# Every third weight remainder of a decoder layer computed on GpSimd instead of VectorE

## The chip, the cores and the metric

The kernel runs on one core of a Trainium2 chip. The metric is the device time of one execution in microseconds (us); less is better. The engines are named as the profile names them: PE (TensorE, matmuls), PEld (its weight loads), DVE (VectorE), ACT (ScalarE), POOL (GpSimd) and SP (SyncE, which issues DMAs here).

## What is computed

One decoder layer on 512 tokens with 2048 channels, all in float32:

```python
xn = rms_norm(x, norm1_g);  proj = xn @ w_in + b_in
mixed = concatenate([conv_group(...), swa_group(...)])     # convolution branch, sliding-window attention
x = x + mixed @ w_out
x = x + peer(rms_norm(x, norm2_g), ...)

def peer(xn, ...):     # 8 heads pick 16 of 16384 one-neuron experts each, for every token
    experts, gates = top-16 of the product keys
    h = einsum("cd,chkd->chk", xc, peer_u[experts])
    a = gelu(h) * gates
    return einsum("chk,chkd->cd", a, peer_v[experts])
```

The expert layer (`peer`) takes most of the time.

## The kernel before, in words

**Two ways through the expert layer.** For 352 of the tokens the kernel computes all 16384 experts densely: a sweep multiplies the activations with `peer_u`, the result is multiplied by gates that are zero for the experts not chosen, and a fold multiplies that with `peer_v` and adds into `acc`. For the other 160 tokens it fetches the chosen expert rows with indirect DMAs that GpSimd issues (`gather`, 320 of them, 1 MB each), and DVE works each fetched row off with one long instruction over 128x2048 elements: L842 for `peer_u`, L859 for `peer_v`. The gathers have three buffers in turn (`grow` twice, and `yrow` or `xrow`), so that gather n may start only when the DVE step of gather n-3 has ended. `step` spreads the gathers over the dense tiles, by number and not by time.

**Weight units.** All dense weights come in 628 units of 128x1024 float32 (512 KB), in a fixed order (`specs`). For each unit `stream` has SP load it (`w_raw`, two buffers; an own queue), ACT round it to the matmul's float32r (`w_hi`, three buffers), and DVE subtract that from the original (`w_lo`, three buffers). So a unit's `w_raw` buffer is free for the unit after next when its `w_lo` is done, and its `w_hi` buffer when PE has used it. PE multiplies each unit with 24 matmuls in the order high weight by high activation, high weight by low activation, low weight by high activation; it needs `w_hi` at the unit's first matmul and `w_lo` at the third. `unit` asks for one unit ahead, and the two instructions of the split stand under a raised priority (400) of the tile scheduler, which sets the order of all instructions on each engine from a simulated timeline.

**Stages of the dense part.** Sweeps 0 to 8 (units 116 to 259) store their results in DRAM. For groups 9 to 15 a sweep of 16 units is followed at once by its fold of 16 units (`fold_group`); the first of these folded groups begins at unit 260. Behind group 15 the stored groups 0 to 8 are folded, 16 units each: `prepare` loads the stored results (`Hb`) and gates (`Gb`), and queues their gating (`gated`, L965, and the split of the gated values at L171 and L172) into the fold of the group before. After each pair of output blocks DVE adds two PSUM banks into `acc` (L989).

Of the kernel before, what the change touches and what calls it, by code (L numbers as in the profile page):

```python
# [9 lines left out]
FT = mybir.dt.float32  # L10
# [4 lines left out]
OP = mybir.AluOpType  # L15
# [11 lines left out]
AHEAD = 9  # L27
START = 10
END = 250.0
PUMP = 5.4  # L30
CONV_K = 31
HD, NQ = 64, 16
NK, PH, TOPK = 128, 8, 16
# [2 lines left out]
C_N1, C_N2, C_CB, C_LG, C_LB, C_BA, C_BG, C_CW = 0, 16, 32, 40, 48, 56, 64, 72  # L36
N_PAR = C_CW + 8 * CONV_K
R_B, R_SK, R_QG, R_KG = 0, 1280, 1296, 1360
# [21 lines left out]
def hymba_layer(ctx: ExitStack, tc: tile.TileContext, xT, pos, par, row, wi, wo, wq, sk, ut, un, vt, vn,  # L60
                out_t, out_r, dbg=None):
    nc = tc.nc
# [18 lines left out]
    def later(cost, fn, *a, low=False):  # L81
        queues[low].append((cost, fn, a))
# [11 lines left out]
    def drain(low=True):  # L94
        for q in queues[:1 + low]:
            while q:
                _, fn, a = q.popleft()
                fn(*a)
# [26 lines left out]
    def stream(upto):  # L125
        while nxt[0] < min(upto, len(specs)):
            i = nxt[0]
            nxt[0] += 1
            raw = raws[-1][0].tile([128, 1024], FT, name="w_raw", bufs=raws[-1][1])
            with tc.high_priority(offset=400 if i >= 4 else 0):  # L130
                nc.sync.dma_start(raw, specs[i])
            hi = ring.tile([128, 1024], FR, name="w_hi", bufs=3)
            lo = ring.tile([128, 1024], FR, name="w_lo", bufs=3)
            with tc.high_priority(offset=400):
                nc.scalar.activation(hi, raw, AF.Copy)  # L135
                nc.vector.tensor_tensor(lo, raw, hi.bitcast(FT), op=OP.subtract)  # L136
            units[i] = (hi, lo)

    def unit(ahead=1):
        i = nxt[1]  # L140
        nxt[1] += 1
        stream(i + 1 + ahead)
        return units.pop(i)
# [19 lines left out]
    def par_col(base, c):  # L163
        return P[:, base + c:base + c + 1]
# [72 lines left out]
    for c in range(KC):  # L237
        if c % 4 == 0:
            stream(c // 4 + 1)
        xr = px.tile([128, T], FT, name="xr", bufs=4)  # L240
        nc.sync.dma_start(xr, xT[c])
        nc.scalar.activation(xh[:, c], xr, AF.Copy, scale=par_col(C_N1, c))
        nc.vector.scalar_tensor_tensor(xl[:, c], xr, par_col(C_N1, c), xh[:, c].bitcast(FT), op0=OP.mult,
                                       op1=OP.subtract)
        if c == 0:
            nc.scalar.activation(ssq, xr, AF.Square)
        else:
            sq = px.tile([128, T], FT, name="sq", bufs=2)
            nc.scalar.activation(sq, xr, AF.Square)
            nc.vector.tensor_tensor(ssq, ssq, sq, op=OP.add)  # L250
# [30 lines left out]
    def conv_chunk(c, h):  # L281
        first = [True]

        def tap(k):
            w = par_col(C_CW, c * CONV_K + k)
            if k == 0:
                nc.vector.tensor_scalar(mix_c[:, c], h[:, :T], w, par_col(C_CB, c), op0=OP.mult, op1=OP.add)
            else:
                nc.vector.scalar_tensor_tensor(mix_c[:, c], h[:, k:k + T], w, mix_c[:, c], op0=OP.mult, op1=OP.add)  # L289
        for k in range(CONV_K):  # L290
            later(0.66, tap, k, low=True)
# [192 lines left out]
    def glu_group(g):  # L484
# [15 lines left out]
        nc.scalar.activation(tg, tg, AF.Sigmoid, bias=par_col(C_BG, g))  # L500
        h = pa_.tile([128, CONV_K - 1 + T], FT, name="h", bufs=2)
        nc.gpsimd.memset(h[:, :CONV_K - 1], 0.0)
        nc.vector.scalar_tensor_tensor(h[:, CONV_K - 1:], ta, par_col(C_BA, g), tg, op0=OP.add, op1=OP.mult)
        conv_chunk(g, h)
# [279 lines left out]
    for h in range(PH):  # L784
# [6 lines left out]
        for u in range(4):  # L791
            hi, lo = unit()
# [123 lines left out]
    def step(first, us):  # L916
        tick[0] += 1
        if tick[0] > START:
            gather_until(int((tick[0] - START) * STEPS / (END - START)) + 1, first)
        pump(us)  # L920
# [18 lines left out]
    for e in range(8 * AHEAD):  # L939
# [3 lines left out]
        if e % 4 == 3:  # L943
            nc.scalar.dma_start(H[e // 4], gl)
        step(first, PUMP)
    drain()
# [149 lines left out]
```

## Time and profile before

| what | value |
|---|---|
| median of three runs | 2863.24 us (2862.2 to 2864.12) |
| the profiled execution | 2863.08 us, of which the span from first to last instruction is 2861.3 us |
| PE busy | 2811.3 us, 98% |
| DVE busy | 2368.2 us, 83% |
| POOL busy | 471.7 us, 16% |
| largest group on DVE | `w_lo`, 628 instructions, 772.1 us |

The span is the profile's own clock; the 1.8 us between it and the execution's time lie around the program. A matmul's rows overlap (each lasts some 0.32 us, and the next starts 0.16 us after it), so a busy PE is read here from its gaps: an idle time of PE or PEld with the name of what ended it.

### The profile page before, as it was taken

To read this page: it belongs to the slowest core of one execution; us is meant where nothing else is said; L and a number is where in the kernel's file an instruction comes from. 1 tells how busy PE (TensorE), PEld (TensorE's weight loads), DVE (VectorE), ACT (ScalarE), POOL (GpSimd) and SP (SyncE) were. 2 spreads that over 40 slices of the span, in tenths; PEclk is the share of its full clock that TensorE was granted. 3 is DMA by queue.
4 is the path that set the end of the run, shared out by engine and by line. 5 is a ranking of instruction groups with operands and counts; after the bars stand their busy time and mean duration, and the time that the engine had idled before them with its cause. 6 is when DMAs were issued, how large, how long until landed. Compare 5 with 4: busy or idle time off the path is not lost. (4 is left out here: it accounts for less than half of the span.)

```text
span 2861.3 us, 43542 instructions
## 1 busy us (share of the span) xinstructions
PE 2811.3 (98%) x16995; PEld 2688.8 (94%) x16995; DVE 2368.2 (83%) x3586; ACT 1214.2 (42%) x1879; POOL 471.7 (16%) x337
## 2 busy tenths in 40 slices
PE   8999999999999999999999999999999999999999
PEld 8998877788899999999999999999999999999999
DVE  7888996569999887777787878878888899997984
ACT  5666434343343787666332333333333333333332
POOL 0000000000002222212212222222222223222320
PEclk9999999999999999999999999999999999999999
DMA  5222332523249999899998989898898999998994
GB/s 174 75 67 74 115 100 85 170 93 136 89 157 345 325 325 339 311 341 339 349 351 321 343 313 359 335 336 336 326 344 323 372 361 350 354 366 329 358 347 147
DMA packets 204207, 764.00 MB, mean 267 GB/s; under 512 B 18593, under 2 KB 70945, under 8 KB 160417
## 3 DMA queue, kind: packets, MB, share of 16 engines
q1 hardware_dynamic: 103584, 378.66, 36.7%
q0 software_dynamic: 46080, 335.56, 31.0%
q10 hardware_dynamic: 54336, 47.00, 5.0%
q8 instruction: 133, 2.18, 0.3%
q14 instruction: 74, 0.60, 0.1%
HBM read 716.42 MB, written 44.70 MB: 266 GB/s over the span
## 5 line engine op out<-in xcount | busy, mean ns | idle before, releaser
L135 ACT ACTIVATE w_hi<-w_raw 128x1024 fp32r<-128x1024 f32 x628 | 666.0, 1061 | 1277.7 <-PE mm L981 536.1
L136 DVE TENSOR_TENSOR w_lo<-w_raw,w_hi 128x1024 fp32r<-128x1024 f32 x628 | 772.1, 1233 | 276.6 <-ACT w_hi L135 275.4
L932 PE MATMUL mm<-nl,w_hi 128*128 128x352 f32 x2048 | 668.2, 326 | 0.0
L930 PE MATMUL mm<-nh,w_hi 128*128 128x352 f32 x2048 | 664.9, 325 | 1.0 <-ACT w_hi L135 1.0
L979 PE MATMUL mm<-ah,w_hi 128*128 128x352 f32 x2048 | 658.4, 323 | 7.4 <-DVE acc L989 7.4
L933 PE MATMUL mm<-nh,w_lo 128*128 128x352 f32 x2048 | 664.0, 325 | 0.0
L981 PE MATMUL mm<-al,w_hi 128*128 128x352 f32 x2048 | 660.3, 323 | 0.0
L982 PE MATMUL mm<-ah,w_lo 128*128 128x352 f32 x2048 | 645.0, 323 | 12.7 <-DVE w_lo L136 12.5
L982 PEld LDWEIGHTS mm<-ah,w_lo 128*128 128x128 f32 x2048 | 380.9, 188 | 18.0 <-DVE w_lo L136 17.9
L979 PEld LDWEIGHTS mm<-ah,w_hi 128*128 128x128 f32 x2048 | 384.0, 188 | 9.2 <-DVE acc L989 7.6
L930 PEld LDWEIGHTS mm<-nh,w_hi 128*128 128x128 f32 x2048 | 385.3, 188 | 1.5 <-ACT w_hi L135 1.3
L933 PEld LDWEIGHTS mm<-nh,w_lo 128*128 128x128 f32 x2048 | 385.4, 188 | 0.1
L932 PEld LDWEIGHTS mm<-nl,w_hi 128*128 128x128 f32 x2048 | 384.8, 188 | 0.1
L981 PEld LDWEIGHTS mm<-al,w_hi 128*128 128x128 f32 x2048 | 384.8, 188 | 0.0
L826 POOL DMA_INDIRECT grow<-un,idx x86 | 121.3, 1411 | 898.9 <-DVE grow L842 591.3
L859 DVE SCALAR_TENSOR_TENSOR yrow<-grow,h,yrow 128x2048 f32<-128x2048 f32 x107 | 251.4, 2349 | 1.5 <-DMA grow<-vn,idxb 1.4
L842 DVE SCALAR_TENSOR_TENSOR grow<-grow,xrow 128x2048 f32<-128x2048 f32 x107 | 244.6, 2286 | 0.8 <-DMA grow<-un,idxb 0.8
L989 DVE TENSOR_TENSOR acc<-acc,mm 128x352 f32<-128x352 f32 x240 | 118.8, 521 | 87.4 <-PE mm L982 87.3
L826 POOL DMA_INDIRECT grow<-vn,idx x85 | 125.4, 1475 | 391.5 <-DVE yrow L859 381.6
L289 DVE SCALAR_TENSOR_TENSOR mix_c<-h,par,mix_c 128x512 f32<-128x512 f32 x240 | 173.8, 750 | 1.6
L859 DVE SCALAR_TENSOR_TENSOR yrow<-xrow,h,yrow 128x2048 f32<-128x2048 f32 x53 | 124.6, 2351 | 0.0
L842 DVE SCALAR_TENSOR_TENSOR yrow<-yrow,xrow 128x2048 f32<-128x2048 f32 x53 | 121.2, 2286 | 2.9 <-DMA xrow<-XB 2.9
(274 smaller groups left out, 3979.3 us busy)
## 6 DMA issues: line engine op xcount, KB each, us to landing
w_raw<-ut SPq DMA_DIRECT2D x256, 512.0 KB
w_raw<-vt SPq DMA_DIRECT2D x256, 512.0 KB
w_raw<-wi SPq DMA_DIRECT2D x52, 512.0 KB
G<-gt ACTq DMA_DIRECT2D x22, 1024.0 KB
Gb<-G SPq DMA_DIRECT2D x16, 1408.0 KB
w_raw<-wo SPq DMA_DIRECT2D x32, 512.0 KB
w_raw<-wq SPq DMA_DIRECT2D x32, 512.0 KB
H<-gl ACTq DMA_DIRECT2D x18, 704.0 KB
```

The costliest lines, as they stand in the source:

```text
L135: nc.scalar.activation(hi, raw, AF.Copy)
L136: nc.vector.tensor_tensor(lo, raw, hi.bitcast(FT), op=OP.subtract)
L289: nc.vector.scalar_tensor_tensor(mix_c[:, c], h[:, k:k + T], w, mix_c[:, c], op0=OP.mult, op1=OP.add)
L826: i = nc.gpsimd.indirect_dma_start(out=g, out_offset=None, in_=src, in_offset=bass.IndirectOffsetOnAxis(ap=at, axis=0))
L842: nc.vector.scalar_tensor_tensor(g, g, 1.0, rows["x"], op0=OP.mult, op1=OP.mult, accum_out=h3[:, k:k + 1])
L859: nc.vector.scalar_tensor_tensor(y, g, h3[:, k:k + 1], y, op0=OP.mult, op1=OP.add)
L930: m = nc.tensor.matmul(bank, hi[:, s], nh[:, k, :TD], start=k == 0, stop=False)
L932: nc.tensor.matmul(bank, hi[:, s], nl[:, k, :TD], start=False, stop=False)
L933: nc.tensor.matmul(bank, lo[:, s], nh[:, k, :TD], start=False, stop=k == KC - 1)
L979: m = nc.tensor.matmul(banks[j], hi[:, ws], ah[:, ee], start=ee == 0, stop=False)
L981: nc.tensor.matmul(banks[j], hi[:, ws], al[:, ee], start=False, stop=False)
L982: nc.tensor.matmul(banks[j], lo[:, ws], ah[:, ee], start=False, stop=ee == 7)
```

## The change

From unit 260 on, the subtraction that makes `w_lo` is issued to GpSimd instead of DVE for every unit whose number divides by three: units 261, 264, ..., 627, which are 123 of the 368 left. Inputs, output and buffers stay the same. The constant is the number of units ahead of the first folded group (116 units of projections, then 16 for each of 9 sweeps).

```diff
+POOL_LO = 116 + 16 * AHEAD
@@ stream
             with tc.high_priority(offset=400):
                 nc.scalar.activation(hi, raw, AF.Copy)
-                nc.vector.tensor_tensor(lo, raw, hi.bitcast(FT), op=OP.subtract)
+                eng = nc.gpsimd if i >= POOL_LO and i % 3 == 0 else nc.vector
+                eng.tensor_tensor(lo, raw, hi.bitcast(FT), op=OP.subtract)
```

Lines behind the first edit move by one, behind the second by two: L826 of before is L828 of the changed kernel, L859 is L861, L965 is L967, L989 is L991.

On POOL, in the folds of the stored groups (units 534 to 546), only gathers stand in a row before; the number behind a name is that of the buffer's use.

```order
L826 DMA xrow_23355<-vn,idx_5227 128x2048
L826 DMA grow_23425<-vn,idx_5227 128x2048
L826 DMA grow_23428<-vn,idx_5227 128x2048
L826 DMA xrow_23498<-vn,idx_5227 128x2048
L826 DMA grow_23568<-vn,idx_5227 128x2048
```

In the changed kernel the same stretch of POOL reads:

```order
L138 TENSOR_TENSOR w_lo_23253<-w_raw_23250,w_hi_23252 128x1024
L828 DMA xrow_23355<-vn,idx_5227 128x2048
L828 DMA grow_23425<-vn,idx_5227 128x2048
L138 TENSOR_TENSOR w_lo_23366<-w_raw_23363,w_hi_23365 128x1024
L828 DMA grow_23428<-vn,idx_5227 128x2048
L828 DMA xrow_23498<-vn,idx_5227 128x2048
L138 TENSOR_TENSOR w_lo_23469<-w_raw_23466,w_hi_23468 128x1024
L828 DMA grow_23568<-vn,idx_5227 128x2048
```

Between two moved subtractions stand about two gathers, and POOL takes all of them in order.

On DVE the scheduler has also put the remaining instructions into another order. Around unit 538 (`w_lo_23396`) in a fold of a stored group, before:

```order
L136 TENSOR_TENSOR w_lo_23366<-w_raw_23363,w_hi_23365 128x1024
L965 TENSOR_TENSOR Hb_23788<-Hb_23788,Gb_23784 128x352 x4
L989 TENSOR_TENSOR acc_13638<-acc_13638,mm_23291 128x352
L989 TENSOR_TENSOR acc_13638<-acc_13638,mm_23292 128x352
L859 SCALAR_TENSOR_TENSOR yrow_17709<-xrow_23355,h3_7322,yrow_17709 128x2048
L965 TENSOR_TENSOR Hb_23790<-Hb_23790,Gb_23784 128x352 x4
L136 TENSOR_TENSOR w_lo_23396<-w_raw_23393,w_hi_23395 128x1024
```

and in the changed kernel, DVE at the same place:

```order
L991 TENSOR_TENSOR acc_13638<-acc_13638,mm_23291 128x352
L991 TENSOR_TENSOR acc_13638<-acc_13638,mm_23292 128x352
L861 SCALAR_TENSOR_TENSOR yrow_17709<-xrow_23355,h3_7322,yrow_17709 128x2048
L138 TENSOR_TENSOR w_lo_23396<-w_raw_23393,w_hi_23395 128x1024
L967 TENSOR_TENSOR Hb_23788<-Hb_23788,Gb_23784 128x352 x4
L967 TENSOR_TENSOR Hb_23790<-Hb_23790,Gb_23784 128x352 x4
```

The subtraction of unit 537 has left DVE, and that of unit 538 now stands ahead of the eight gating instructions.

Where the folds of the stored groups begin (units 474 to 476), DVE before:

```order
L136 TENSOR_TENSOR w_lo_21094<-w_raw_21091,w_hi_21093 128x1024
L172 TENSOR_TENSOR al_20908<-Hb_20909,ah_20907 128x352
L859 SCALAR_TENSOR_TENSOR yrow_17709<-grow_21050,h3_7322,yrow_17709 128x2048
L172 TENSOR_TENSOR al_20908<-Hb_20909,ah_20907 128x352
L172 TENSOR_TENSOR al_20908<-Hb_20911,ah_20907 128x352 x4
L989 TENSOR_TENSOR acc_13638<-acc_13638,mm_21059 128x352
L136 TENSOR_TENSOR w_lo_21134<-w_raw_21131,w_hi_21133 128x1024
L989 TENSOR_TENSOR acc_13638<-acc_13638,mm_21060 128x352
L859 SCALAR_TENSOR_TENSOR yrow_17709<-xrow_21053,h3_7322,yrow_17709 128x2048
L136 TENSOR_TENSOR w_lo_21164<-w_raw_21161,w_hi_21163 128x1024
```

and in the changed kernel:

```order
L861 SCALAR_TENSOR_TENSOR yrow_17709<-grow_21050,h3_7322,yrow_17709 128x2048
L174 TENSOR_TENSOR al_20908<-Hb_20909,ah_20907 128x352
L174 TENSOR_TENSOR al_20908<-Hb_20911,ah_20907 128x352 x4
L991 TENSOR_TENSOR acc_13638<-acc_13638,mm_21059 128x352
L861 SCALAR_TENSOR_TENSOR yrow_17709<-xrow_21053,h3_7322,yrow_17709 128x2048
L138 TENSOR_TENSOR w_lo_21134<-w_raw_21131,w_hi_21133 128x1024
L991 TENSOR_TENSOR acc_13638<-acc_13638,mm_21060 128x352
L138 TENSOR_TENSOR w_lo_21164<-w_raw_21161,w_hi_21163 128x1024
```

Unit 474's subtraction (`w_lo_21094`) is gone from DVE, and unit 475's (`w_lo_21134`) now stands behind one more of the long gather steps.

## Rows read from the trace of the kernel before

**Rows 1.** The page's first part: busy us, share of span and instructions by engine.

```profile
PE 2811.3 (98%) x16995; PEld 2688.8 (94%) x16995; DVE 2368.2 (83%) x3586; ACT 1214.2 (42%) x1879; POOL 471.7 (16%) x337
```

**Rows 2.** Busy time in five stretches: length, PE, PEld, DVE, ACT, POOL, clock, DMA.

```profile
1400.00:2240.00 840.00, 833.84 (x5206) 832.39 (x5205) 674.43 (x671) 280.36 (x344) 182.29 (x143) 1.00 0.90 338
1800.00:1900.00 100.00, 100.00 (x627) 100.00 (x627) 81.15 (x84) 33.62 (x42) 21.58 (x17) 1.00 0.90 340
2240.00:2275.00 35.00, 31.65 (x191) 30.25 (x191) 35.00 (x40) 9.38 (x10) 11.91 (x6) 1.00 0.95 370
2275.00:2700.00 425.00, 414.34 (x2560) 410.15 (x2559) 377.88 (x396) 133.68 (x163) 125.23 (x71) 1.00 0.92 354
2700.00:2861.00 161.00, 156.76 (x963) 154.50 (x961) 115.29 (x109) 45.28 (x50) 26.16 (x19) 1.00 0.71 261
```

**Rows 3.** Waits from 1400 to 2240 us: us in total, times, longest.

```profile
PEld mm L979 <- DVE acc L989: 7.6, 5, 2.0
```

**Rows 4.** Waits from 2240 to 2275 us.

```profile
PEld mm L982 <- DVE w_lo L136: 3.2, 4, 1.7
PEld mm L979 <- ACT w_hi L135: 1.5, 1, 1.5
```

**Rows 5.** Waits from 2275 to 2700 us.

```profile
DVE acc L989 <- PE mm L982: 39.0, 22, 6.7
PEld mm L982 <- DVE w_lo L136: 14.7, 14, 1.6
DVE w_lo L136 <- ACT w_hi L135: 6.6, 9, 2.2
DVE yrow L859 <- DMA grow<-vn,idxb: 1.4, 2, 1.2
```

**Rows 6.** Groups on DVE, 2240 to 2861 us: busy, mean ns, idle before.

```profile
L136 DVE TENSOR_TENSOR w_lo<-w_raw,w_hi 128x1024 fp32r<-128x1024 f32 x154 | 186.3, 1224 | 26.6 <-ACT w_hi L135 26.5
L859 DVE SCALAR_TENSOR_TENSOR yrow<-grow,h,yrow 128x2048 f32<-128x2048 f32 x65 | 152.8, 2351 | 1.5 <-DMA grow<-vn,idxb 1.4
L989 DVE TENSOR_TENSOR acc<-acc,mm 128x352 f32<-128x352 f32 x157 | 78.1, 522 | 57.6 <-PE mm L982 57.6
L859 DVE SCALAR_TENSOR_TENSOR yrow<-xrow,h,yrow 128x2048 f32<-128x2048 f32 x32 | 75.3, 2353 | 0.0
L172 DVE TENSOR_TENSOR al<-Hb,ah 128x352 fp32r<-128x352 f32 x71 | 32.3, 522 | 0.0
L965 DVE TENSOR_TENSOR Hb<-Hb,Gb 128x352 f32<-128x352 f32 x64 | 29.5, 529 | 0.0
```

**Rows 7.** Timeline about 1797 us: start, length, instruction, [idle before, releaser].

```profile
1796.48 1.23 DVE L136 TENSOR_TENSOR w_lo<-w_raw,w_hi 128x1024 fp32r<-128x1024 f32 x1 [0.40 <-ACT w_hi L135]
...
1803.18 0.19 PEld L933 LDWEIGHTS mm<-nh,w_lo 128*128 128x128 f32 x1
```

**Rows 8.** Timeline about 2497 us, a late unit.

```profile
2496.79 1.83 DVE L965 TENSOR_TENSOR Hb<-Hb,Gb 128x352 f32<-128x352 f32 x4
...
2499.81 0.30 PEld L982 LDWEIGHTS mm<-ah,w_lo 128*128 128x128 f32 x2 [0.66 <-DVE w_lo L136]
```

**Rows 9.** Groups on POOL, the whole span: two MEMSET sizes.

```profile
L855 POOL MEMSET yrow<- 128x2048 f32 x1 | 1.8, 1812 | 10.9 <-DMA out_r<-yrow 10.9
L348 POOL MEMSET vh<- 128x1024 f32 x1 | 1.0, 954 | 40.0 <-PE rowstat L262 40.0
```

**Rows 10.** Timeline about 2315 us, POOL and DVE.

```profile
2314.47 2.35 DVE L859 SCALAR_TENSOR_TENSOR yrow<-xrow,h,yrow 128x2048 f32<-128x2048 f32 x1
2314.71 2.93 POOL L826 DMA_INDIRECT grow<-vn,idx  x1 [4.45 <-DVE yrow L859]
```

**Rows 11.** Timeline about 2434 us, POOL and the DVE instruction behind.

```profile
2433.84 0.94 POOL L826 DMA_INDIRECT grow<-vn,idx  x1 [3.71 <-DVE yrow L859]
2435.84 0.52 DVE L989 TENSOR_TENSOR acc<-acc,mm 128x352 f32<-128x352 f32 x1 [2.27 <-PE mm L982]
```

**Rows 12.** Waits of SP's queue, 2240 to 2861 us.

```profile
SPq L131 <- DVE w_lo L136: 432.6, 150, 8.7
```

## The prediction

> **What bounds the kernel now.** I read the page's first part, then the stretches, then who waited for whom in each, and only then single places. PE is busy for 2811.3 of 2861.3 us [rows 1]. The stretch from 1800 to 1900 us shows what a PE without gaps looks like: 627 matmuls in 100.00 us [rows 2], 0.16 us each, so a unit of 24 takes 3.83 us and three units take 11.5 us. Nothing done on another engine makes that faster; the change can only take away gaps of PE, or add some. The reader should see how few there are behind 1400 us, where the moved units begin: 7.6 us for `acc` [rows 3], 3.2 and 1.5 us from 2240 to 2275 us [rows 4], 14.7 us in 14 waits from 2275 to 2700 us [rows 5]. From 2700 us on DVE makes PE wait no more; its last gaps belong to the program's end. The waits that carry the name of `w_lo` sum up to 17.9 us in 18 waits, 0.6% of the time. That is about the ceiling of a gain.
>
> They all lie in the folds of the stored groups. In the folded groups ahead, `w_lo` is ready long before its use: at 1797 us it starts right when ACT's `w_hi` ends, is done at 1797.71, and PE first loads it at 1803.18 [rows 7], 5.5 us later. From 2240 to 2275 us DVE is busy for all of 35.00 us, from 2275 to 2700 us for 377.88 of 425 us, 89% [rows 2]. Its queue is in order, and a `w_lo` that stands behind gating or a gather step there comes late: at 2497 us four gating instructions, 1.83 us, run right ahead of unit 538's `w_lo`, and PE waits 0.66 us [rows 8].
>
> **What the change removes.** DVE loses one `w_lo` of 1224 ns [rows 6] in three units: 123 of them, 37 in the 425 us (425 / 11.5). With nothing added, DVE's 377.88 us there would be 333.
>
> **What it adds on GpSimd.** The trace has no GpSimd instruction with two inputs. The nearest rows are the two MEMSETs, 954 ns for 1024 elements in a partition and 1812 ns for 2048 [rows 9]: 858 ns for each 1024 elements that go one way, and 96 ns around. Two inputs read one after the other give 96 + 2 x 858 = 1.8 us, two inputs and the output one after the other 2.7 us. I take 2.2 us, between the ends, since no row tells which is nearer. The Trainium skill has a figure, in "GPSIMD Engine Reference", section 3.1: 4497 ns for an addition over 2048 elements, from which half, 2.25 us, is an estimate; by it the sum would not change.
>
> POOL works 125.23 of the 425 us now [rows 2], so 37 x 2.2 = 81 us more fit. What counts is its order: a moved subtraction stands behind a gather that may wait for a DVE step, and gathers stand behind a subtraction that waits for `w_hi`. Reading each moved unit against the trace of before (the later of `w_hi`'s end and the end of the gather ahead of it, plus 2.2 us) leaves at most units some 4 us before PE needs them; for about five of the 49 or so units from 2240 to 2800 us it leaves nothing or up to a microsecond. I take +1 us for those. Gathers move back by up to 2.2 us or what the subtraction waits; DVE waited only 1.4 us for gathered data in the late stretch [rows 5], so their cover is thin but there, and I take nothing for them. SP's next load waits for `w_lo` as well, 150 times [rows 12]; at 1797 us a GpSimd subtraction would end 1 us after DVE's. That load is for the unit after next, which PE reaches two units or 7.7 us later, so nothing is taken for it either.
>
> **What it costs DVE.** Does a GpSimd instruction that reads two tensors hold DVE up? The trace shows the other direction. A gather issue takes 0.94 us when DVE is idle [rows 11] and 2.93 us when it starts 0.24 us into a long gather step; that step ends at 2316.82, and the issue ends 0.82 us after that [rows 10]. So a GpSimd instruction is held while a DVE instruction with two SBUF inputs runs. How a long reading instruction of GpSimd holds DVE is not shown; the ends are nothing, and its whole length. I take the whole length, for the share of time in which DVE has such an instruction: all groups of [rows 6] but `acc` (whose second input is in PSUM), 186.3 + 152.8 + 75.3 + 32.3 + 29.5 = 476 of 621 us, 77%. Then one moved subtraction costs DVE 0.77 x 2.2 = 1.7 us and saves 1.22: +0.5 us net, with ends of -1.2 and +1.5 (2.7 without any cover). Times 37 that is +18 us: DVE at 396 of 425 us, 93%.
>
> The Trainium skill speaks against the change here: "SBUF — State Buffer", the practical consequences in its table of ports, says that a DVE instruction with two SBUF inputs and a GpSimd instruction that reads SBUF exclude each other, and that whichever comes second is blocked until the first has ended. The trace agrees in the one direction that it shows, 2.93 against 0.94 us. By the rule the sum is the one below; without it, it is the first rival's.
>
> **What the new order does.** DVE's order in the late stretch changes by more than the missing instructions. Adding up the DVE work ahead of each remaining `w_lo` in both orders, with the durations of [rows 6], the eleven late units from 2275 to 2700 us that stay on DVE fare so: ten stand earlier by 0.9 to 5.7 us, mostly by one gather step (2.35 us) or a little more, one stands where it stood. The place at unit 538 is of this kind: the eight gating instructions now come behind its `w_lo`. The other three late units go to GpSimd. Against that, a half to one net microsecond of blocking in a run of DVE between two idle times (31 idle times in 425 us, one in 13.7 us, so about one GpSimd instruction in each run) rarely eats 2.35 us. So of the 14.7 us I count 14 as gone.
>
> Three other units (491, 550, 554) stand later by 2.3 to 6.6 us and had slack of 2.3 to 5.5 us: +2 us. Units nearly late before get the 0.5 us on top: +1 us. In the opening part, 2240 to 2275 us, DVE has no idle time, and units 475 and 479 each get one gather step of 2.35 us more ahead of them, while two or three blocked subtractions cost 0.5 us net each. PE waits once for both (the second delay falls into the first): +3 us, on top of the 3.2 that stay.
>
> The waits of 7.6 us for `acc` [rows 3] come from loads of the residual; they stay.
>
> **Sum.** -14 (late units from 2275 to 2700 us) + 3 (opening part) + 2 (units put later) + 1 (nearly late) + 1 (GpSimd's own) = -7 us. The profiled execution took 2863.08 us, 0.16 us under the median, so the forecast is 2856 us.
>
> **Rivals.** *No blocking.* If DVE runs on beside GpSimd, every moved subtraction is a gain of 1.2 us for DVE: the opening part costs +1 instead of +3, the nearly late units nothing and the units put later +1: -14 + 1 + 1 + 1 = -11 us, and with half of the 3.2 us of [rows 4] gone as well, about -13: 2850 us. For it speaks that the rows show only GpSimd waiting; against it that the held issue shows a shared resource.
>
> *The relief is eaten.* The net +0.5 us falls on units that have no slack, mostly in long runs of DVE without idle time, where four GpSimd instructions add 2 us: half of the 14 us stays, and the sum is 0: 2863 us, within 6 us either way. For it speaks that DVE stays at 93%.
>
> *DVE becomes the bound from 2275 to 2700 us* (the slower side). DVE has 47 us to spare there, 1.27 us for each of the 37 subtractions. If one costs more than that net, that is over 2.5 us of blocked DVE each, as with a GpSimd instruction of 2.7 us or more and no cover, DVE needs all of the 425 us, and the idle times in which it waits for PE (39.0 us [rows 5]) can't all be filled. With 2.7 us, full blocking adds 1.5 x 37 = 55 us, 8 more than are free; if a quarter of the 47 us can't be filled, PE waits 20 us instead of 14.7, and with the opening part's +5 and late GpSimd units the time is about 2875 us; a GpSimd instruction of 3 us would give near 2890. For it speaks that GpSimd's duration is unmeasured; against it that the early idle time and the new order give some back.
>
> *The change doesn't do what it says*: the built program has 123 subtractions on POOL, so this is out.
>
> **Chances.** Forecast (3 to 11 us faster) 0.32; no blocking 0.18; relief eaten 0.27; DVE as the bound 0.23. 0.2% is 5.7 us, about what a measurement of this kernel can tell from no change. Of the forecast's 0.32 some 0.28 lie beyond that on the fast side and 0.04 within; relief eaten lies within but for 0.03 on the slow side; no blocking is fast, 0.18. So faster 0.46, within 0.28, slower 0.26. The range reaches from the no-blocking case with something to spare to the point where DVE is just the bound: 2846 to 2877 us. The forecast's own range is 2852 to 2860 us.
>
> **What would show it.** POOL should have 123 subtractions of about 2.2 us, and some longer by what a DVE instruction ahead of them still had to run. DVE's long gather steps or `w_lo` should at times last up to 2.2 us more, or start late behind nothing; if all keep 2.35 and 1.22 us, there is no blocking. The waits of PE for `w_lo` from 2275 to 2700 us should fall from 14.7 to some 4 us, and those in the opening part rise from 3.2 to about 6. I am wrong if waits for GpSimd's `w_lo` show in the folded groups ahead of 2240 us, where 5.5 us should cover everything, if DVE waits for gathers by more than 10 us, or if DVE's idle time from 2275 to 2700 us is used up.

## The result, and the profile after

The changed kernel takes 2898.97 us (median of four executions, 2892.07 to 2902.36) beside 2862.72 us of the kernel before on the same chip: a ratio of 1.0126, with an interval of 1.0111 to 1.014. It is 36 us slower. The forecast was 2856 us, faster, with a range up to 2877 us; both its sign and its range were wrong. The profiled execution took 2897.86 us, its span is 2896.0 us, 34.7 us over the span of before.

The first part of the page, busy us by engine, answers to [rows 1]:

```profile
PE 2828.0 (98%) x16995; PEld 2705.3 (93%) x16995; DVE 2383.0 (82%) x3463; ACT 1210.5 (42%) x1879; POOL 863.7 (30%) x460
```

DVE issues 123 instructions fewer and is busy for 15 us *more*. PE is busy for 17 us more at the same 16995 matmuls. Neither can come from the work itself, which is the same.

Where the time goes is seen best over the same work, since a kernel that has fallen behind does other work in the same microseconds. The matmuls of the stretches of [rows 2] (1400 to 2240 us, 2240 to 2275, 2275 to 2700, and from there on) are found again by counting matmuls from the start. In the changed kernel they take these stretches (columns as there):

```profile
1402.30:2242.90 840.60, 835.25 (x5206) 833.93 (x5205) 669.32 (x591) 274.40 (x335) 429.52 (x214) 1.00 0.89 337
2242.90:2291.80 48.90, 36.34 (x191) 35.21 (x190) 44.56 (x46) 13.37 (x18) 18.86 (x11) 0.86 0.83 316
2291.80:2732.90 441.10, 420.36 (x2561) 417.24 (x2560) 391.19 (x358) 133.68 (x163) 219.79 (x105) 0.98 0.90 336
2732.90:2896.00 163.10, 157.47 (x962) 154.33 (x960) 112.03 (x97) 44.87 (x50) 70.20 (x32) 1.00 0.71 257
```

The folded groups take 0.6 us more than before, the opening part 48.9 instead of 35 us, the late stretch 441 instead of 425, the end 163 instead of 161. Some 2 us of the 34.7 lie ahead of 1402 us, where GpSimd has not begun its first subtraction (1407.0 us).

The waits of PE's weight loads in the opening part and in the late stretch (columns as in [rows 3]: us in total, times, longest):

```profile
PEld mm L984 <- DVE w_lo L138: 8.8, 3, 5.5
PEld mm L981 <- ACT ah L173: 4.9, 1, 4.9
...
PEld mm L984 <- DVE w_lo L138: 20.8, 8, 4.8
PEld mm L984 <- POOL w_lo L138: 3.1, 3, 1.4
```

Against [rows 4] (4.7 us) the opening part now has 13.7 us, and the late stretch 23.9 us against the 14.7 of [rows 5]. The shape changed too: fourteen waits of at most 1.6 us became eight for DVE's `w_lo`, the longest 4.8 us, and three for GpSimd's. The end has 1.8 us for `w_lo`, where before it made PE wait for nothing. The folded groups have 6.7 us against 7.6 [rows 3], none of it for `w_lo`. All in all the waits for operands behind 1400 us rose from 27.0 to 46.2 us, by 19.2 us.

That leaves 15 of the 34.7 us. The stretches of time (columns as in [rows 2]) around seven of the longer waits show the larger part of them:

```profile
1537.40:1540.80 3.40, 3.38 (x11) 3.38 (x12) 2.62 (x3) 0.00 (x0) 0.00 (x0) 0.50 1.04 422
2247.40:2254.20 6.80, 5.86 (x20) 5.88 (x21) 6.80 (x12) 2.79 (x4) 1.73 (x1) 0.50 0.79 285
2278.10:2284.90 6.80, 5.32 (x18) 5.32 (x19) 4.82 (x4) 0.00 (x0) 3.77 (x2) 0.50 0.97 378
2332.70:2339.50 6.80, 5.72 (x19) 5.72 (x20) 4.75 (x4) 0.00 (x0) 2.70 (x2) 0.50 0.84 316
2397.50:2400.90 3.40, 3.03 (x10) 3.04 (x11) 3.40 (x5) 0.00 (x0) 0.00 (x0) 0.51 0.99 347
2476.10:2479.50 3.40, 3.40 (x13) 3.40 (x13) 2.73 (x2) 0.00 (x0) 1.53 (x1) 0.51 0.98 377
2595.50:2598.90 3.40, 2.79 (x9) 2.80 (x10) 3.40 (x3) 0.00 (x0) 0.00 (x0) 0.50 0.99 400
```

In these seven stretches, 34.0 us together, TensorE was granted half its clock (0.50: 1.2 instead of 2.4 GHz). Each begins during or right behind a wait of PE of 2.3 to 5.5 us. At half the clock the matmuls follow each other every 0.29 us instead of 0.16. The seven stretches hold 100 of them: 100 x 0.13 = 13 us. The kernel before has no such stretch behind 1400 us; its longest wait there is 2.0 us [rows 3], and its granted clock reads 1.00 in every stretch of [rows 2].

So the 34.7 us are 19.2 of waits, 13 of matmuls at half the clock, and 2.5 that I don't assign, nearly all of it the 2 us ahead of the first moved unit.

**What makes `w_lo` late.** The added group on POOL and the groups on DVE behind 1400 us (busy us, mean ns of one, idle before):

```profile
L138 POOL TENSOR_TENSOR w_lo<-w_raw,w_hi 128x1024 fp32r<-128x1024 f32 x123 | 365.4, 2971 | 385.4 <-ACT w_hi L136 384.7
```

```profile
L138 DVE TENSOR_TENSOR w_lo<-w_raw,w_hi 128x1024 fp32r<-128x1024 f32 x244 | 327.4, 1349 | 90.5 <-ACT w_hi L136 81.9 <-issue 8.5
L861 DVE SCALAR_TENSOR_TENSOR yrow<-grow,h,yrow 128x2048 f32<-128x2048 f32 x107 | 285.2, 2666 | 9.1 <-DMA grow<-vn,idx 7.2 <-DMA yrow<-YB 1.0 <-DMA grow<-vn,idxb 0.7
L861 DVE SCALAR_TENSOR_TENSOR yrow<-xrow,h,yrow 128x2048 f32<-128x2048 f32 x53 | 139.2, 2627 | 1.9 <-DMA xrow<-vn,idx 1.6
L991 DVE TENSOR_TENSOR acc<-acc,mm 128x352 f32<-128x352 f32 x232 | 113.2, 515 | 88.6 <-PE mm L984 88.3
L967 DVE TENSOR_TENSOR hv<-hv,Gb 128x352 f32<-128x352 f32 x56 | 60.1, 1075 | 7.8 <-ACT hv L936 7.7
L174 DVE TENSOR_TENSOR al<-hv,ah 128x352 fp32r<-128x352 f32 x56 | 44.0, 787 | 19.8 <-ACT ah L173 19.8
L967 DVE TENSOR_TENSOR Hb<-Hb,Gb 128x352 f32<-128x352 f32 x72 | 42.3, 649 | 7.6 <-DMA Gb<-G 7.6
```

Against [rows 6], `w_lo` went from 1224 to 1349 ns, the gather steps from some 2350 to 2666 and 2627, `Hb` from 529 to 649. Only `acc`, whose second input lies in PSUM, kept its length (522 to 515). One place shows how it happens; the timeline about 2275 us, with start, length and, in brackets, the idle time before:

```profile
2271.58 4.55 DVE L967 TENSOR_TENSOR Hb<-Hb,Gb 128x352 f32<-128x352 f32 x4
...
2272.02 2.41 POOL L138 TENSOR_TENSOR w_lo<-w_raw,w_hi 128x1024 fp32r<-128x1024 f32 x1
...
2276.05 2.34 DVE L861 SCALAR_TENSOR_TENSOR yrow<-xrow,h,yrow 128x2048 f32<-128x2048 f32 x1
2278.31 2.35 DVE L138 TENSOR_TENSOR w_lo<-w_raw,w_hi 128x1024 fp32r<-128x1024 f32 x2
...
2279.58 0.50 PEld L984 LDWEIGHTS mm<-ah,w_lo 128*128 128x128 f32 x2 [5.51 <-DVE w_lo L138]
```

Four gating instructions, 1.83 us in [rows 8], last 4.55 us, because a subtraction of 2.41 us on GpSimd begins just behind the first of them. The gather step and the `w_lo` behind them keep their own lengths, but start 2.7 us later, and PE waits for that `w_lo`, unit 479's, for 5.51 us. The first of the two `w_lo` ends at about 2279.5, when PE goes on, after 1.2 us. This hold is not alone: DVE has had no idle time for 37 us by then, and in that run of work GpSimd has held it twice more (gating at 2242 us by 2.2 us, a `w_lo` at 2258.55 us that took 3.97 us).

### The profile page after: what moved, and what is told of

Same layout as the page of the kernel before. It is cut to its first block, busy times and chain, and to the rows that moved or that the text cites. A ratio compares the mean times of both kernels' runs of the same rounds, so it can differ in the third digit from the quotient of the medians.

```text
span 2896.0 us, 43552 instructions
## 1 busy us (share of the span) xinstructions
PE 2828.0 (98%) x16995; PEld 2705.3 (93%) x16995; DVE 2383.0 (82%) x3463; ACT 1210.5 (42%) x1879; POOL 863.7 (30%) x460
## 5 line engine op out<-in xcount | busy, mean ns | idle before, releaser
L138 DVE TENSOR_TENSOR w_lo<-w_raw,w_hi 128x1024 fp32r<-128x1024 f32 x505 | 647.0, 1285 | 247.1 <-ACT w_hi L136 236.3
L138 POOL TENSOR_TENSOR w_lo<-w_raw,w_hi 128x1024 fp32r<-128x1024 f32 x123 | 365.4, 2971 | 385.4 <-ACT w_hi L136 384.7
L828 POOL DMA_INDIRECT grow<-un,idx x86 | 128.5, 1494 | 787.3 <-DVE grow L844 479.1
L861 DVE SCALAR_TENSOR_TENSOR yrow<-grow,h,yrow 128x2048 f32<-128x2048 f32 x107 | 285.2, 2666 | 9.1 <-DMA grow<-vn,idx 7.2
L844 DVE SCALAR_TENSOR_TENSOR grow<-grow,xrow 128x2048 f32<-128x2048 f32 x107 | 248.4, 2323 | 5.8 <-DMA grow<-un,idx 5.5
L991 DVE TENSOR_TENSOR acc<-acc,mm 128x352 f32<-128x352 f32 x240 | 117.2, 515 | 102.7 <-PE mm L984 102.5
L828 POOL DMA_INDIRECT grow<-vn,idx x85 | 124.0, 1459 | 140.3 <-DVE yrow L861 120.4
L861 DVE SCALAR_TENSOR_TENSOR yrow<-xrow,h,yrow 128x2048 f32<-128x2048 f32 x53 | 139.2, 2627 | 1.9 <-DMA xrow<-vn,idx 1.6
```

The lines of the kernel that those rows point to most:

```text
L138: eng.tensor_tensor(lo, raw, hi.bitcast(FT), op=OP.subtract)
L828: i = nc.gpsimd.indirect_dma_start(out=g, out_offset=None, in_=src, in_offset=bass.IndirectOffsetOnAxis(ap=at, axis=0))
L844: nc.vector.scalar_tensor_tensor(g, g, 1.0, rows["x"], op0=OP.mult, op1=OP.mult, accum_out=h3[:, k:k + 1])
L861: nc.vector.scalar_tensor_tensor(y, g, h3[:, k:k + 1], y, op0=OP.mult, op1=OP.add)
```

## The experiments

The theory (blocking): a GpSimd instruction that reads two tensors from SBUF and a DVE instruction with two SBUF inputs can't run together, so each moved subtraction holds DVE, and the loss comes from what stands behind the held instruction. The rivals: the new order on DVE, later gathers, later loads, or GpSimd being late with its own results.

**The relief alone.** In the changed kernel the moved subtraction is left out; the unit takes the low half of the unit before it, so the output is not the layer's.

```diff
-                eng = nc.gpsimd if i >= POOL_LO and i % 3 == 0 else nc.vector
-                eng.tensor_tensor(lo, raw, hi.bitcast(FT), op=OP.subtract)
+                if i >= POOL_LO and i % 3 == 0:
+                    lo = units[i - 1][1] if i - 1 in units else last_lo[0]
+                else:
+                    nc.vector.tensor_tensor(lo, raw, hi.bitcast(FT), op=OP.subtract)
```

> The 123 moved subtractions are left out altogether (those units use the low half of the unit before, so their products are not the reference's); everything else is as in the changed kernel, and DVE is as free of them, but GpSimd gets none. Theory A (GpSimd's subtraction blocks DVE's two-input instructions for its whole length): without it the relief remains alone, the waits of PE for w_lo behind 1400 us fall under the 17.9 us of before, DVE's gather steps stay at 2.35 us, and the time is about 2850 us (-0.4%). Theory B (the new order of DVE and SP that the scheduler made, not the blocking, makes w_lo and the gates late): the time stays above 2875 us.

Measured: 2852.75 us, ratio 0.9967 (0.9953 to 0.9981), with every length on DVE as before. So taking the work from DVE is worth about 10 us when nothing is put elsewhere. The waits for `w_lo` from 2275 to 2700 us fall to about half, and not at the same units: with the units counted in order, those that were late before have 0.9 us left, and the rest lies at units that were not late before, such as 491, 506 and 554:

```profile
PEld mm L989 <- DVE w_lo L142: 7.8, 9, 1.5
```

**The subtraction on GpSimd without the relief.** DVE keeps all its work, and GpSimd does every third subtraction once more into a scratch tile that nobody reads.

```diff
                 nc.vector.tensor_tensor(lo, raw, hi.bitcast(FT), op=OP.subtract)
+                if i >= POOL_LO and i % 3 == 0 and scr:
+                    nc.gpsimd.tensor_tensor(scr[0], raw, hi.bitcast(FT), op=OP.subtract)
```

> The kernel before, with DVE doing all subtractions, plus on GpSimd the same subtraction once more for every third unit from the first folded group on, into a scratch tile that nothing reads. Theory A (blocking): each of the 123 costs DVE some 1.2 us in stretched instructions and nothing is saved, DVE is full behind 2275 us, and the time is above that of the changed kernel, 2900 to 2960 us. Theory B (order): DVE's order is near that of before, so the time is within 8 us of 2863 us. Theory C (moved units come late because GpSimd's own queue is late): nothing waits for GpSimd here but the reuse of w_raw, so 2863 to 2872 us.

Measured: 2948.19 us, ratio 1.0302 (1.0285 to 1.0319). The groups on POOL, then those on DVE behind 1400 us:

```profile
L140 POOL TENSOR_TENSOR scr<-w_raw,w_hi 128x1024 f32<-128x1024 f32 x123 | 393.6, 3200 | 285.8 <-ACT w_hi L137 278.1 <-issue 6.8
```

```profile
L138 DVE TENSOR_TENSOR w_lo<-w_raw,w_hi 128x1024 fp32r<-128x1024 f32 x369 | 543.8, 1485 | 50.0 <-ACT w_hi L137 48.1 <-issue 1.4
L863 DVE SCALAR_TENSOR_TENSOR yrow<-grow,h,yrow 128x2048 f32<-128x2048 f32 x107 | 291.5, 2724 | 0.2
L995 DVE TENSOR_TENSOR acc<-acc,mm 128x352 f32<-128x352 f32 x240 | 116.2, 511 | 46.2 <-PE mm L988 46.0
```

No DVE instruction was moved away, yet `w_lo` lasts 1485 ns and the gather steps 2724, with `acc` unchanged. An instruction whose result nobody uses costs 86 us. One thing does wait for its end: SP, before it loads into `w_raw` again (110 us in 41 waits). But ACT waited for loaded weights for 58 us behind 1400 us, against 69 us before, so later loads are not what costs: the running of the subtraction harms, not its result. (The scheduler has also changed DVE's order here, so not all of the 86 us need be blocking.)

**GpSimd busy without reading.** The kernel before, with three MEMSETs on GpSimd for every third unit, which only write.

```diff
+                if i >= POOL_LO and i % 3 == 0 and scr:
+                    for w in (1024, 1024, 512):
+                        nc.gpsimd.memset(scr[0][:, :w], 0.0)
```

> The kernel before, plus on GpSimd three MEMSETs (1024, 1024 and 512 elements in a partition, about 0.95 + 0.95 + 0.53 = 2.4 us by the MEMSET rows) for every third unit from the first folded group on, into a scratch tile that nothing reads: as much GpSimd time as a subtraction, in the same queue as the gathers, but nothing read. DVE's order is that of before but for three places. Theory A with reads as the cause: DVE's instructions keep their lengths, 2860 to 2868 us. If any GpSimd work blocks DVE, or if gathers put back by it are the cause: above 2880 us.

Measured: 2883.18 us, ratio 1.0087 (1.0054 to 1.0119). DVE's groups behind 1400 us, and its waits from 1400 to 2240 us:

```profile
L138 DVE TENSOR_TENSOR w_lo<-w_raw,w_hi 128x1024 fp32r<-128x1024 f32 x369 | 447.3, 1220 | 106.7 <-ACT w_hi L137 106.3
L864 DVE SCALAR_TENSOR_TENSOR yrow<-grow,h,yrow 128x2048 f32<-128x2048 f32 x107 | 250.9, 2345 | 2.0 <-DMA grow<-vn,idxb 1.1 <-issue 0.8
```

```profile
DVE grow L847 <- DMA grow<-un,idx: 25.2, 11, 3.4
...
DVE grow L847 <- DMA grow<-un,idxb: 18.5, 12, 2.9
```

All lengths are those of before, so writing GpSimd instructions don't hold DVE. They waited for nothing, though, and the scheduler set them all early: the 369 MEMSETs run from 1418 to 1857 us, mostly six to eight and once fourteen in a row between two gathers, and none in the folds of the stored groups, which the next experiment covers. The loss of 21 us arose in the folded groups: the gathers came late, DVE waited for gathered data (25.2 and 18.5 us in the rows, and 18.4 in two smaller ones), and PE waited for `w_lo` for 12.4 us ahead of 2240 us, where it waited for none before. That is a price of a busy GpSimd queue that the prediction set at nothing, and it puts the time where the expectation had it for late gathers. In the changed kernel it is smaller: the gather steps at L861 shown above wait 7.2 + 0.7 + 1.6 us.

**Same place, same wait, no reading.** The changed kernel with a MEMSET of `w_lo` in place of the subtraction; it waits for `w_hi` too. The low halves of these units are zero.

```diff
-                nc.scalar.activation(hi, raw, AF.Copy)
+                act = nc.scalar.activation(hi, raw, AF.Copy)
+                if i >= POOL_LO and i % 3 == 0:
+                    m = nc.gpsimd.memset(lo.bitcast(FT), 0.0)
+                    tc.add_manual_dep(m.ins, act.ins.name, ...)
```

> The changed kernel with the moved subtraction replaced by a GpSimd MEMSET of w_lo (0.95 us) that waits for w_hi as the subtraction does: same units, same place in GpSimd's queue with its gathers, w_lo still comes from GpSimd, DVE has the same relief, but nothing is read from SBUF (the low half of those units is zero, so that part of the products is left out). Theory A (reads block): DVE's instructions keep 1.22 and 2.35 us and the time is near the run without the subtraction, 2848 to 2858 us. Theory C (GpSimd's queue: w_lo behind waiting gathers, gathers behind waiting w_lo): PE waits for w_lo from POOL remain and the time is above 2870 us.

Measured: 2856.48 us, ratio 0.9976 (0.9961 to 0.9991). The waits of PE from 2275 to 2700 us, and the lengths on DVE behind 1400 us:

```profile
PEld mm L989 <- DVE w_lo L143: 7.1, 8, 1.5
PEld mm L989 <- POOL w_lo L138: 3.1, 4, 1.6
```

```profile
L143 DVE TENSOR_TENSOR w_lo<-w_raw,w_hi 128x1024 fp32r<-128x1024 f32 x247 | 301.6, 1224 | 156.0 <-ACT w_hi L136 150.1 <-issue 4.7 <-PE mm L940 1.2
L972 DVE TENSOR_TENSOR hv<-hv,Gb 128x352 f32<-128x352 f32 x56 | 29.1, 521 | 11.7 <-ACT hv L941 9.0 <-DMA Gb<-G 2.7
```

This kernel has the removed DVE work and an instruction on GpSimd at each of the 123 places, with the same wait for `w_hi` and the gathers behind it, and it is faster than before. What differs from the changed kernel is that the GpSimd instruction reads nothing and is shorter (957 ns), and two things that follow: DVE's instructions are again in another order, and SP may load into `w_raw` as soon as `w_hi` is done, since the MEMSET doesn't read it. So this run does not rule out by itself that later loads make `w_lo` late. The waits of ACT for loaded weights from 2240 us on, in the kernel before and in the changed one, do:

```profile
ACT w_hi L135 <- DMA w_raw<-vt: 60.5, 17, 5.3
```

```profile
ACT w_hi L136 <- DMA w_raw<-vt: 21.7, 6, 4.3
```

They fell. The 42 us between the two kernels are the price of GpSimd's reading and its length, with what the order adds.

**One input instead of two.** The changed kernel with a GpSimd copy of `w_hi` in place of the subtraction; the low halves are wrong by that.

```diff
+                if i >= POOL_LO and i % 3 == 0:
+                    nc.gpsimd.tensor_copy(lo, hi.bitcast(FT))
```

> The changed kernel with the moved subtraction replaced by a GpSimd copy of w_hi into w_lo: one SBUF input instead of two (the low half of those units is a copy of the high half, so their products are not the reference's). Theory A: a GpSimd read blocks DVE's two-input instructions for as long as it lasts; a copy should last about 1.0 to 1.3 us, half of the subtraction's 2.42, and each stretches a DVE instruction by half as much, so DVE gains 0.6 us net for each unit and the waits and the clock's stretches shrink: 2852 to 2872 us. If only instructions of GpSimd with two inputs block, as e6: 2848 to 2858 us.

> The copy in place of the subtraction once more (the low half of those units is a copy of the high half), for a profile. Theory A: GpSimd's copy lasts 1.0 to 1.3 us when nothing is in its way, and DVE's w_lo and gather steps are stretched by about half of what the subtraction stretches them, the sum over 1400 us on near 75 us instead of 152.

Measured: 2867.88 us, ratio 1.0018 (1.0002 to 1.0033). The lengths are from an execution of 2867.47 us. The copy takes 1.05 us where nothing holds it and 1521 ns in the mean. DVE's `w_lo` last 1247 ns and its `hv` gating 710 (521 with the MEMSET). So the copy holds DVE too, but less, by some 33 us in all, under half of the 75 that I expected. The three kernels stand in the order of what GpSimd reads, and of how long its instruction lasts: nothing 2856, one tensor 2868, two tensors 2899 us.

**Only the early, only the late units.**

```diff
-                eng = nc.gpsimd if i >= POOL_LO and i % 3 == 0 else nc.vector
+                eng = nc.gpsimd if POOL_LO <= i < 474 and i % 3 == 0 else nc.vector
```

> The change for units 261 to 471 alone (folded groups, before the stored groups are folded); from unit 474 on all subtractions are on DVE. Theory A: DVE is blocked here as well, but w_lo has 5.5 us of slack, so little of the loss arises here: 2858 to 2872 us. Theory B (order, at the change from folded to stored groups): about half of the loss stays, 2875 to 2885 us.

Measured: 2868.93 us, ratio 1.0018 (1.0004 to 1.0032), with 71 subtractions.

> The change for units 474 to 627 alone (52 subtractions, from the folds of the stored groups on). In the run with units 261 to 471 alone the loss was 0.2%, some 6 us. Theory A (blocking where w_lo has no slack): nearly the whole loss arises here, 2884 to 2896 us, with waits of PE for w_lo of 25 us or more and stretches of half clock behind the long ones. If the loss comes from a backlog that the folded groups hand over, 2865 to 2875 us.

Measured: 2888.7 us, ratio 1.0082 (1.0053 to 1.0111), with 52 subtractions (`i >= 474`). The 71 in the folded groups, where `w_lo` has 5.5 us to spare [rows 7], cost some 6 us (none of it in waits for `w_lo`, which stay at 17.9 us; a late `ah` and `acc` and 10 us at half the clock are behind it). The 52 in the folds of the stored groups bring some 27 of the 36 us.

**Gathers spread sooner.** In the kernel before, the last gathers are set for tick 240 instead of 250 of the dense work, so that less of the long steps is left for the end.

```diff
-END = 250.0
+END = 240.0
```

> The kernel before with one number changed: the gathers are spread to tick 240 instead of 250, so that 4% more gather steps stand in the folded groups, where DVE has idle time, and fewer in the folds of the stored groups. If the waits for w_lo of before (17.9 us) come from DVE's load there: a few us less, 2850 to 2860 us. If they come from the order in the queue alone: 2860 to 2868 us.

Measured: 2873.27 us, ratio 1.0031 (1.0018 to 1.0044). PE's waits for `w_lo` came to 21.9 us in 17 waits with one of 4.3 us, so spreading the gathers sooner is no remedy. Both expectations were too low; why it is slower than before was not followed further.

**More slack for `w_lo`.** A fourth buffer of `w_hi` and `w_lo` in the folds of the stored groups, and one more unit asked for ahead; first on the kernel before, then on the changed one.

```diff
-            hi = ring.tile([128, 1024], FR, name="w_hi", bufs=3)
-            lo = ring.tile([128, 1024], FR, name="w_lo", bufs=3)
+            pool, n = (ring2[0], 1) if ring2 and i % 4 == 3 else (ring, 3)
+            hi = pool.tile([128, 1024], FR, name="w_hi", bufs=n)
+            lo = pool.tile([128, 1024], FR, name="w_lo", bufs=n)
-        stream(i + 1 + ahead)
+        stream(i + 1 + ahead + len(ring2))
```

> The kernel before with one more buffer of w_hi and of w_lo (four instead of three) and one unit more asked for ahead, once the last sweep has freed the room, that is in the folds of the stored groups alone; DVE makes all subtractions. Theory A (the waits there are single late w_lo's measured against 5.5 us of slack, not a lack of DVE time): the slack grows by a unit, 3.8 us, nearly all of the 17.9 us of waits go, 2844 to 2852 us. If DVE's time is what is short: no change, 2858 to 2866 us.

> The changed kernel (every third subtraction on GpSimd) with the same additional buffer in the folds of the stored groups. Theory A: the blocking stays, DVE's instructions are stretched as before, but waits of up to 5.5 us shrink to 1.7 us or nothing, and stretches of half clock behind them go; most of the loss from unit 474 on (27 us by the run of the late units alone) goes: 2860 to 2875 us. If the blocking makes DVE short of time: 2885 to 2900 us.

Measured: on the kernel before 2854.62 us, ratio 0.9975 (0.9967 to 0.9984), the fastest full kernel of this study, though PE's waits for `w_lo` only fell from 17.9 to 13.3 us and did not nearly go. On the changed kernel 2888.34 us, ratio 1.0091 (1.007 to 1.0111): some 10 us better than without, but no rescue, and in the range expected if blocking made DVE short of time. Short of time it is not: over the work of the late stretch it is idle for 54 of 441 us. The timeline of the latter about 2580 us, ACT, DVE and POOL, shows why:

```profile
2570.24 1.06 ACT L137 ACTIVATE w_hi<-w_raw 128x1024 fp32r<-128x1024 f32 x1 [3.54 <-DMA w_raw<-vt]
```

```profile
2576.66 1.82 DVE L968 TENSOR_TENSOR Hb<-Hb,Gb 128x352 f32<-128x352 f32 x4
...
2581.53 5.03 DVE L139 TENSOR_TENSOR w_lo<-w_raw,w_hi 128x1024 fp32r<-128x1024 f32 x2
```

```profile
2581.98 2.35 POOL L139 TENSOR_TENSOR w_lo<-w_raw,w_hi 128x1024 fp32r<-128x1024 f32 x1
```

Counting the units in order, the `w_lo` that starts at 2581.53 belongs to the `w_hi` that ended at 2571.30. As far as `w_hi` goes it could have run ten us sooner, but DVE's queue holds gating, a gather step and `acc` ahead of it; then it is itself held (the two `w_lo` of the last DVE row take 5.03 instead of 2.4 us) by the subtraction on POOL, and PE waits 4.8 us. A buffer more gives ACT its head start, not DVE, whose order stands in the program.

**The same reading in shorter pieces.** The changed kernel with each moved subtraction as two instructions of 512 columns.

```diff
-                eng.tensor_tensor(lo, raw, hi.bitcast(FT), op=OP.subtract)
+                for s in ((slice(0, 512), slice(512, 1024)) if eng is nc.gpsimd else (slice(0, 1024),)):
+                    eng.tensor_tensor(lo[:, s], raw[:, s], hi[:, s].bitcast(FT), op=OP.subtract)
```

> The changed kernel with each moved subtraction cut into two instructions of GpSimd, columns 0 to 511 and 512 to 1023, so GpSimd reads as much as in the changed kernel, in pieces half as long. If the harm comes from single DVE instructions that are held for up to the length of a GpSimd instruction just ahead of a w_lo that PE needs, a DVE instruction can get in between the halves: the longest stretch of a w_lo falls from 2.7 to about 1.4 us, PE's waits for DVE's w_lo behind 1400 us fall from 30 to some 20, few waits are long enough for TensorE's clock to be granted at half, and the time is 2865 to 2882 us. If the sum of the time in which GpSimd reads decides, DVE is held as long as before, in other portions, GpSimd is itself held at twice as many places, and the time stays at 2890 to 2910 us.

Measured: 2900.05 us, ratio 1.0132 (1.0112 to 1.0152), the same as the changed kernel. The finer form of my theory, that the length of a single held burst decides, falls. The timeline about 2280 us, DVE and POOL:

```profile
2277.22 1.82 DVE L968 TENSOR_TENSOR Hb<-Hb,Gb 128x352 f32<-128x352 f32 x4
2278.96 3.38 DVE L862 SCALAR_TENSOR_TENSOR yrow<-xrow,h,yrow 128x2048 f32<-128x2048 f32 x1
2282.27 3.42 DVE L139 TENSOR_TENSOR w_lo<-w_raw,w_hi 128x1024 fp32r<-128x1024 f32 x2
```

```profile
2277.66 5.81 POOL L139 TENSOR_TENSOR w_lo<-w_raw,w_hi 128x512 fp32r<-128x512 f32 x2
```

The two engines alternate: the first half waits for the gating, the gather step for the first half (3.38 instead of 2.35 us), the second half for the gather step, and the `w_lo` behind for the second half (3.42 for two instead of 2.4). DVE loses 2 us in a row all the same, in two portions instead of one, and PE waited 4.3 us for this `w_lo`. Over the whole kernel, 5 of the 160 gather steps of `peer_v` were stretched by over 1.5 us, against 21 with whole subtractions, but `w_lo` lasted 1411 ns in the mean against 1349; the sum of the stretches hardly changed.

## Why the prediction was wrong, step by step

**What bounds the kernel** was right: PE does, and all of the change shows as gaps of PE. But the ceiling of a gain, 17.9 us, was matched by no floor for the loss.

**The cost on GpSimd** was nearly right: 2.40 us where nothing holds it (taken: 2.2), 2.97 in the mean, since DVE holds it too. Its own lateness, forecast at +1 us, was 4.3 us of PE's time.

**The cost on DVE** was right in kind and somewhat too high in size. Blocking goes both ways, as "SBUF — State Buffer" of the Trainium skill says in the consequences of its table of ports; the trace now shows both directions, DVE's `w_lo` at up to 3.97 us instead of 1.22. From the six groups with two SBUF inputs shown above, against the lengths of [rows 6] and of the MEMSET kernel, and three smaller ones with 11 us, DVE was held for some 145 us, 1.2 us for each of the 123 subtractions, where I had taken 1.7. (Where DVE keeps all its work it is more: in the kernel without the relief, by the 261 ns of 369 `w_lo`, the 373 of 107 gather steps and the other groups, some 219 us or 1.8 each.) In the late stretch DVE is busy for 391.19 us over the work that took it 377.88 us before [rows 2]: 13 us more, where the sum had 18. It has some 50 us of idle time there, as before. DVE did not become the bound, as the slower rival had it. The time was lost all the same, which neither the forecast nor that rival's mechanism contained.

**The step that failed** is the price of blocking for a single unit: "a half to one net microsecond of blocking in a run of DVE between two idle times", about one GpSimd instruction in each run. It set a mean against units that have no slack. With the units counted in order on DVE and POOL, each term can be held against its waits:

| term | forecast, us | waits, us |
|---|---|---|
| fourteen late units from 2275 to 2700 us | -14 | 14.7 became 1.7, 1.4 of it at unit 486, now on GpSimd |
| opening part | +3 | +9, and 5 at half the clock |
| units put later (491, 550, 554) | +2 | 4.1 + 1.6 + 4.8 = 10.6 |
| units nearly late before: those that became late (506, 526, 553, 584, two small ones) | +1 | 10.6 |
| GpSimd's own (486, 528, 588, 594) | +1 | 4.3 |

So the term of -14 came true, and the other four were too small. Together, with unit 486 counted once, they make 20 us of added waits instead of a gain of 7 us. The terms for units on DVE were priced with a net half microsecond for each hold, or with none. A hold puts up to 2.75 us on one DVE instruction, the 1.22 us that are saved mostly fall elsewhere, and holds add up: ahead of the `w_lo` of units 479, 506, 526 and 554 DVE ran for 27 to 45 us without idle time, with two to four held instructions that lost 4.2 to 8.8 us together. Unit 554, with three of them:

```profile
2566.25 5.05 DVE L174 TENSOR_TENSOR al<-Hb,ah 128x352 fp32r<-128x352 f32 x8
...
2576.61 4.64 DVE L861 SCALAR_TENSOR_TENSOR yrow<-xrow,h,yrow 128x2048 f32<-128x2048 f32 x1
...
2592.16 5.03 DVE L138 TENSOR_TENSOR w_lo<-w_raw,w_hi 128x1024 fp32r<-128x1024 f32 x2
...
2596.10 0.50 PEld L984 LDWEIGHTS mm<-ah,w_lo 128*128 128x128 f32 x2 [4.82 <-DVE w_lo L138]
```

The eight `al` take some 3.6 us, the gather step 2.35 and two `w_lo` 2.4 us when nothing holds them.

The new order has a share in these waits. Without reading on GpSimd, PE still waits for the same units: with the MEMSET 2.6 us at unit 479, 1.5 at 491 and 1.4 at 506, and in the relief alone 2.9, 1.5 and 1.5, and 1.4 at 554. In the changed kernel it is 5.5, 4.1, 3.7 and 4.8 us. DVE's orders in these kernels differ in places, so the split between order and hold is not exact.

**The opening part** was forecast at +3 us by way of late `w_lo`. It is +14 over the same work: 9 us of waits, and 5 us lost on 38 matmuls at half the clock. Units 475 and 479 are late, as forecast, but by 2.5 and 5.5 us, and ahead of them stands another wait. `Gb`, the gates, is loaded later, and the gating that needs it is held as well. In the kernel before, and in the changed one:

```profile
2235.25 3.58 DVE L965 TENSOR_TENSOR Hb<-Hb,Gb 128x352 f32<-128x352 f32 x8 [3.61 <-DMA Gb<-G]
```

```profile
2242.03 5.73 DVE L967 TENSOR_TENSOR Hb<-Hb,Gb 128x352 f32<-128x352 f32 x8 [7.60 <-DMA Gb<-G]
...
2244.55 2.39 POOL L138 TENSOR_TENSOR w_lo<-w_raw,w_hi 128x1024 fp32r<-128x1024 f32 x1 [14.37 <-ACT w_hi L136]
...
2248.31 0.29 PEld L981 LDWEIGHTS mm<-ah,w_hi 128*128 128x128 f32 x1 [4.86 <-ACT ah L173]
```

The eight gating instructions wait 7.60 instead of 3.61 us for `Gb` and last 5.73 instead of 3.58 us, with a subtraction of GpSimd among them; the `ah` that PE needs is late by 4.86 us. Loads were taken at nothing; this one was not: SP issued it 2.65 us later, and why it then took 4 us longer to land is open.

**The clock** was in no term. 13 of the 34.7 us between the two profiled executions are matmuls at half the clock, at or behind the long waits. In the kernel with gathers spread sooner, the one wait of over 2 us, 4.3 us long at 2256 us, lies at a stretch of half the clock of 6.8 us; a second one of 3.4 us, at 2496 us, follows waits of only 0.7, 0.3 and 1.8 us. The MEMSET kernel has two of 3.4 us, behind waits of 3.5 and 2.6 us. The waits of before (2.0 us) and of the relief alone (2.8 us) have none. The size of one wait does not decide it by itself: in the kernel before with more slack a wait of 3.5 us had none either, and behind the changed kernel's waits of 2.5 us at 2258 and 2.7 us at 2716 no further stretch began.

**What I said would prove me wrong** came in part. PE's waits for `w_lo` rose in the late stretch, where they should have fallen to some 4 us. No wait for GpSimd's `w_lo` showed ahead of 2240 us, and DVE's idle time was not used up. But DVE waited for gathered data for 24 us behind 1400 us (9.5 at L861, 14.9 at L844, the steps of `peer_u`); all but 0.7 us of it lies ahead of 2240 us, where no wait of PE for `w_lo` shows.

**Two statements to mend.** `w_raw` has four buffers from line 593 of the kernel before on (`raws.append((rawp, 4))`), not two as the section on the kernel says; the load behind a `w_lo` is for the unit four later. The conclusion drawn from it, that later loads of weights cost nothing, holds: ACT waits less for loaded weights than before, as the two rows under the MEMSET in place show. And the end of the kernel, from 2700 us on in the kernel before, was left out of the sum; it costs 2 us.

**The rivals.** "No blocking", with 2850 us, is what the chip does if GpSimd doesn't read: 2853 to 2856 us. "The relief is eaten" came nearest to what happens, long runs of DVE without idle time with up to four GpSimd instructions in them, but priced four at 2 us; in the four runs above two to four cost 4.2 to 8.8 us. "DVE becomes the bound" had the right side, and 2875 to 2890 us, but neither its mechanism nor enough of it.

## What to carry to other kernels

An elementwise instruction on GpSimd that reads SBUF is not free work beside a DVE that lives on two-input instructions: it took DVE about as much time (1.2 us) as it relieved it of (1.22 us), and some of it right ahead of a `w_lo` for which PE then waited. Don't weigh a mean gain against a mean cost where a queue in order feeds an engine without slack; ask which single instructions are held, how many of them one run without idle time collects, what stands behind them, and how long PE then waits. A gap of some microseconds on PE can cost more than itself, since the clock may fall behind it; one more buffer for the split in the folds, without GpSimd, gave 0.25%.

## What was not expected of the hardware

At or behind seven waits of 2.3 to 5.5 us, though not at every one of that size, TensorE was granted half its clock for 3.4 or 6.8 us. A GpSimd MEMSET (957 ns for 128x1024, and up to fourteen in a row) lengthens no DVE instruction, a GpSimd copy of the same size (1.05 us) does by some 0.3 us in the mean, a subtraction (2.40 us) by 1.2 us in the mean and up to 2.75 us. And cutting the GpSimd instruction in halves did not shrink the hold: the two engines took turns, and DVE lost as much.
